# Value columns leave the seven-product stage normalised, as two planes of 16-bit words that are transposed by DMA when a head loads them

## The chip, the cores and the metric

The kernel runs on one core of a Trainium2 chip. The metric is the device time of one execution in microseconds (us). The core has five engines with queues of their own: TensorE (PE in the profile; its weight loads are PEld), VectorE (DVE), ScalarE (ACT), GpSimd (POOL) and SyncE (SP). An instruction waits at the head of its engine's queue until the semaphores that it names are reached, and what stands behind it waits too. Data moves between DRAM and the on-chip memory SBUF by DMA, which SP, ACT and POOL issue; TensorE's results lie in PSUM.

## The reference

One decoder layer on 1024 tokens of width 2048: a norm, an input projection, eight heads of stick-breaking and eight of differential attention, each gated, an output projection, a gated embedding and a last norm. What the change touches is the norm and the columns v and g:

```python
def rmsnorm(x, g, eps=NORM_EPS):
    xf = x.astype(jnp.float32)
    y = xf * lax.rsqrt(jnp.mean(xf * xf, axis=-1, keepdims=True) + eps)
    return (y * g.astype(jnp.float32)).astype(x.dtype)
...
        hn = rmsnorm(h, norm_mix_g[i])
        proj = hn @ w_in[i]
        sb_q, sb_k, sb_v, sb_g, df_q, df_k, df_v, df_g = jnp.split(proj, split_at, axis=-1)
...
        sb_out = stick_breaking_attention(sb_q.reshape(sb_shape), sb_k.reshape(sb_shape),
                                          sb_v.reshape(sb_shape)).reshape(B, S, SB_WIDTH)
...
        mixed = jnp.concatenate([sb_out * jax.nn.silu(sb_g), df_out * jax.nn.silu(df_g)], axis=-1)
```

The factor rsqrt(mean of squares) belongs to a token, so it can be multiplied into a projected column after the product.

## The kernel before

Products are made in float32 precision from pairs: every operand is split into a high part, rounded to TensorE's float format (a copy on ScalarE), and the rest (a subtraction on VectorE), and each 128x128 by 128x512 product takes three passes: high by high, high by low, low by high. "High" and "low" below mean these parts.

**The v and g columns** (4096 of the 8192) are computed first, transposed: a unit u is one head, with 128 columns of v and 128 of g, for two halves of 512 tokens. This 2x2 block product is made with seven products instead of eight, named by their operands: A11, A12, S2, S1, S3, A22, S4 (class `Seven`, L656). The x operands (tiles cA11, cS2 and so on, 512 tokens wide) stay for all units; the weights' sums (T1 to T4, L760) are made for each unit on VectorE, then rounded on ScalarE (L801) and their low parts taken on VectorE (L815), one weight for each product made, in a fixed order (`step`). The contraction over 2048 runs in two passes: `ph` 0 takes half of x's rows for all 16 units, `ph` 1 the other half. In the first pass, the A11 and A12 products of all units come first, by themselves, up to about 95 us; then 16 units of five products, to about 312 us; then the second pass, 16 units of seven, to about 613 us. A unit's results are sums (s1, u2, u3: L1145 to L1170) and come out as four tiles of 128 columns by 512 tokens, for token halves `hf` and for v (`blk` 0) or g (`blk` 1). `vput` (L913) stores them on GpSimd's DMA queue into vg_d; in the second pass that DMA adds to what lies there. So vg_d ends with unnormalised v and g, columns on partitions. `prod` (after each product) also runs small pieces of other work from a list `gv.xq`, each from a given slot (number of products) on, two or three at most for a product.

**Visits.** Behind each of the first four units of the first pass, `visit(i)` (L997) loads four x tiles `xv` of the other half of x's rows (both token halves of two blocks) and leaves their combinations in DRAM for the second pass, in two pieces: `one` (slot + 3) scales a tile on ScalarE (L1014) and makes two combinations, `two` (slot + 5) two more. The four tiles are those of a ring, so a visit's loads, on SyncE's queue, wait until the stores of the visit before have landed.

**Row sums of squares.** In every second unit of the second pass, `squares` (L1050) loads four x tiles on ScalarE's DMA queue and, in two pieces, squares them on ScalarE and adds them into `ssa`, one tile for each token half (L1066). The sums over partitions are made later, in the first steps of the attention stage: `split_sum` (L1223) and `norms` (L1210), with four ssps products, a logarithm and an exponential for each half (`rstd_from`, L113) and three VectorE rows, which leave the factor in `ssa`, the same in each partition.

**Attention** runs over half 1 and then half 0 of the tokens, and over 16 heads in each. For each head a stream of projection products for q and k (L294 to L296, accumulators acc) runs on TensorE with the pieces of attention between them; a counter `side` decides after which product a piece is issued (the table TICK). `load_vg` (L1441) loads vf and gf, 256 KB each, from vg_d; `normed(0)` and `normed(1)` multiply them by the factor (L1464); `values` (L465) transposes vf on TensorE in four blocks of 128 tokens (vps, L472), and makes v's high part (L474, ScalarE) and low part (L477, VectorE). The softmax weights are transposed by TensorE too (tp, L492), split into high and low (lead, awh, awl), and multiplied with v (av).

The two pieces of a visit, and the transposes of v, are these:

```python
            def one():
                A.activation(b2, b2, AF.Copy, scale=gcol(kb))
                V.scalar_tensor_tensor(b2, a2, gcol(ka), b2, op0=ALU.mult, op1=ALU.add)
                store("S1", b2)
                V.tensor_tensor(a2, a2, a1, op=ALU.subtract)
                store("S3", a2)
...
            for j in range(4):
                T.transpose(vps[:, j, :], vg[0][:, j * P:(j + 1) * P], ident)
```

Of the kernel before, what the change touches and what calls it, by code (L numbers as in the profile page):

```python
# [15 lines left out]
BF16 = mybir.dt.bfloat16  # L16
AF = mybir.ActivationFunctionType
# [28 lines left out]
    (1, 2), "kv": 9, "df_vg": (25, 37, 42, 58, 59.5), "sb_vg": (4, 15, 16, 24, 25.5), "q_turn": (-1.0, 5.5, 5, 6.5, 10, 12,  # L46
# [22 lines left out]
def _body(ctx, nc, tc, ap):  # L69
# [236 lines left out]
    vg_d = dram.tile([2, 2, NVG, P, HALF], F32, name="vg_d", tag="vg_d")  # L306
    h_d = dram.tile([2, NK, P, HALF], F32, name="h_d", tag="h_d")
# [37 lines left out]
    def attention(at, pz, half, hd, q, qz, K, KL, VV, sg, vg, rcol):  # L345
# [119 lines left out]
        def values():  # L465

            if sb:
                vps = pz.tile([P, 8, P], F32, name="vps", tag="z")[:, 0:4, :]
            else:
                vps = pp.tile([P, 4, P], F32, name="vps", tag="t")  # L470
            for j in range(4):
                T.transpose(vps[:, j, :], vg[0][:, j * P:(j + 1) * P], ident)  # L472
            v = at.tile([P, 2, 4, P], F32R, name="v", tag="v")
            side.later(TICK["vparts"][0], lambda: A.copy(v[:, 0], vps))  # L474

            def low():
                V.tensor_tensor(v[:, 1], vps, v[:, 0].bitcast(F32), op=ALU.subtract)  # L477
# [154 lines left out]
    with tc.tile_pool(name="at", bufs=2) as at, tc.tile_pool(name="pz", bufs=2, space=PSUM) as pz:  # L632
# [370 lines left out]
        def visit(i):  # L1003
# [8 lines left out]

            def one():
                A.activation(b2, b2, AF.Copy, scale=gcol(kb))  # L1014
                V.scalar_tensor_tensor(b2, a2, gcol(ka), b2, op0=ALU.mult, op1=ALU.add)
# [10 lines left out]
            return one, two  # L1026
# [26 lines left out]
        def squares(n):  # L1053
            ts = []
            for j in range(4):
                t = spare()
                A.dma_start(t, xsrc(j % 2, 2 * n + j // 2))
                ts.append(t)

            def some_of(j0):  # L1060
                for j in (j0, j0 + 1):
                    if n == 0 and j < 2:
                        A.activation(ssa[j % 2], ts[j], AF.Square)
                    else:
                        A.activation(ts[j], ts[j], AF.Square)
                        V.tensor_tensor(ssa[j % 2], ssa[j % 2], ts[j], op=ALU.add)  # L1066

            return partial(some_of, 0), partial(some_of, 2)
# [57 lines left out]
        def rest_of(st_, first):  # L1126
# [6 lines left out]
            vput(o, ph, hf, blk, u)  # L1133
# [3 lines left out]
        for ph in range(2):  # L1137
            for u in range(NVG):
# [69 lines left out]
        rstds = {}  # L1208

        def norms():  # L1210
            t = ev.tile([P, HALF], F32, name="ssq", tag="ssq")
            for hf in (1, 0):
                ps = pp.tile([P, HALF], F32, name="ssps", tag="t")
                high, low = halves[hf]
                T.matmul(ps, onesr, high, start=True, stop=False)
                T.matmul(ps, onesr, low, start=False, stop=True)
                side.later(1 if hf else 3, partial(rstd_from, ps, 1.0 / NK, eps6, EPS, ssa[hf], t))
                rstds[hf] = ssa[hf]
            with tc.issue_after(gv.lastx.ins):
                consts_late()  # L1220

        halves = {}

        def split_sum(hf):
            high, low = halves[hf] = [ev.tile([P, HALF], F32R, name=nm, tag="xt", bufs=4) for nm in ("ssah", "ssal")]
            A.copy(high, ssa[hf])
            V.tensor_tensor(low, ssa[hf], high.bitcast(F32), op=ALU.subtract)

        side.add([(14 - hf, partial(split_sum, hf)) for hf in (1, 0)] + [(18, norms)])
# [199 lines left out]
        for half in (1, 0):  # L1429
            X = X0 if half == 0 else X1  # L1430

            for hd in ORDER:
# [8 lines left out]
                def load_vg(vg=vg, hd=hd, half=half):  # L1441
                    for i in range(2):
                        vg.append(f32t(("vf", "gf")[i]))
                        nc.sync.dma_start(vg[i], vg_d[half, i, hd])
# [101 lines left out]
                if half == 0:  # L1546
# [3 lines left out]
                    def load_kv(k2=k2, v2=v2, KL=KL, hd=hd):  # L1550
                        G.dma_start(k2.rearrange("p a b -> p (a b)"), k_d[hd])
                        if hd >= H:
# [7 lines left out]
                                                   (load_vg, partial(normed, 0), partial(normed, 1), gate, gated))])  # L1560
# [877 lines left out]
```

## Time and profile before

| | |
|---|---|
| three runs | 2318.01, 2314.68, 2315.53 us, median 2315.53 |
| span of the profiled execution, first to last instruction | 2312.5 us |
| its own time, with some 3 us around the span | 2315.5 us |
| granted TensorE clock, mean | 0.999 |
| busy in the span: TensorE, VectorE, ScalarE, GpSimd | 100%, 78%, 55%, 14% |
| DMA traffic | 556.66 MB, mean 241 GB/s |

A row of a timeline gives the start in us, the duration in us, engine, source line, operation, output<-inputs, shape and count, and in brackets the idle time of the engine just before and what ended it. A group row gives minimum, median and maximum duration in ns, and the first and last start. Matmuls overlap in the array: starts are 0.23 us apart where each shows 0.39. VectorE's and ScalarE's rows overlap by some 0.1 us as well, so the start of the next row tells what one costs its engine.

### The profile page before, as it was taken

How to read it: one execution, taken by the hardware profiler on the slowest of the kernel's cores; microseconds unless marked ns; L12 is line 12 of the kernel's file. 1: busy time of each engine (PE TensorE's matmuls, PEld its weight loads, DVE VectorE, ACT ScalarE, POOL GpSimd, SP SyncE). 2: the span in 40 equal slices, each digit the busy share in tenths (PEclk: the TensorE clock that was granted, in tenths of full speed). 3: DMA queues.
4: the chain of work that ended last, by engine and by line, in shares of the span. 5: the costliest groups of instructions: out<-in, count | busy, mean ns of one | idle time of the engine just before them, and what ended most of it. 6: DMA issues, size and time to landing. Idle time of an engine off the chain costs nothing.

```text
span 2312.5 us, 32656 instructions
## 1 busy us (share of the span) xinstructions
PE 2301.0 (100%) x11089; PEld 1928.8 (83%) x11089; DVE 1800.0 (78%) x3123; ACT 1273.0 (55%) x2308; POOL 329.8 (14%) x498
## 2 busy tenths in 40 slices
PE   9999999999999999999999999999999999999998
PEld 7888888888888888888888888888888888888887
DVE  6587776766678888878778878788887988687887
ACT  6423243433356677778776766667733435542555
POOL 2121111111211111101011001110121121111000
PEclk9999999999999999999999999999999999999999
DMA  7687788876887787889676667777899789998975
GB/s 268 215 296 234 253 280 226 213 160 131 207 273 253 244 255 247 252 286 309 196 214 188 184 202 210 203 203 241 264 214 246 248 246 283 308 354 275 301 259 187
DMA packets 258455, 556.66 MB, mean 241 GB/s; under 512 B 28896, under 2 KB 39392, under 8 KB 258288
## 3 DMA queue, kind: packets, MB, share of 16 engines
q1 hardware_dynamic: 180816, 366.55, 49.9%
q0 software_dynamic: 60912, 158.10, 26.1%
q10 hardware_dynamic: 16560, 29.92, 3.5%
q8 instruction: 87, 1.43, 0.2%
q14 instruction: 80, 0.66, 0.1%
HBM read 359.16 MB, written 203.69 MB: 243 GB/s over the span
## 4 chain that ended last, share of the span: by engine, by line
PE 97%; DVE 1%; issue 0%; ACT 0%; DMA 0%; SPq 0%; DVEq 0%; ACTq 0%
PE pbc L706 14%; PE pa L706 11%; PE acc L294 10%; PE acc L296 10%; PE acc L295 10%; PE pc L706 9%; PE pb L706 4%; PE tp L492 3%; PE pb L1856 2%; PE pb L1854 2%; PE pb L1855 2%; PE av L539 1%; PE z L386 1%; PE z L385 1%; PE av L538 1%; PE av L537 1%
## 5 line engine op out<-in xcount | busy, mean ns | idle before, releaser
L801 ACT CAST wpr<-T 128x512 fp32r<-128x512 f32 x208 | 127.1, 621 | 469.0 <-DVE T L760 392.9
L294 PE MATMUL acc<-xh,whi 128*128 128x512 f32 x768 | 312.3, 407 | 0.0
L296 PE MATMUL acc<-xh,wlo 128*128 128x512 f32 x768 | 301.1, 392 | 0.0
L295 PE MATMUL acc<-xl,whi 128*128 128x512 f32 x768 | 300.7, 392 | 0.0
L296 PEld LDWEIGHTS acc<-xh,wlo 128*128 128x128 f32 x768 | 144.2, 188 | 32.3 <-DVE wlo L195 0.2
L294 PEld LDWEIGHTS acc<-xh,whi 128*128 128x128 f32 x768 | 144.7, 188 | 24.2
L295 PEld LDWEIGHTS acc<-xl,whi 128*128 128x128 f32 x768 | 144.9, 189 | 23.7
L914 POOL DMA_DIRECT2D vg_d<-hc x128 | 89.8, 701 | 444.8 <-DVE hc L1132 263.2
L815 DVE TENSOR_TENSOR wpr<-T,wpr 128x512 fp32r<-128x512 f32 x208 | 142.7, 686 | 7.2 <-ACT wpr L801 4.2
L199 ACT CAST whi<-wraw 128x1024 fp32r<-128x1024 f32 x128 | 134.1, 1048 | 17.0 <-DMA wraw<-w_in 7.6
L801 ACT CAST wpr<-wraw 128x512 fp32r<-128x512 f32 x128 | 78.7, 618 | 103.6 <-DMA wraw<-tw_d 33.7
L441 ACT ACTIVATE et<-z,mx 128x512 f32<-128x512 f32 (+7 forms) x128 | 95.2, 744 | 59.1 <-DVE mx L433 58.9
L433 DVE CUSTOM_DVE_ANT_0 z<-z,wide 128x512 f32<-128x512 f32 (+7 forms) x128 | 97.7, 765 | 32.7 <-PE z L386 29.3
L516 DVE TENSOR_TENSOR awl<-tp,awh 128x256 fp32r<-128x256 f32 (+1 forms) x160 | 92.6, 579 | 32.6 <-ACT awh L511 31.7
L706 PE MATMUL pbc<-cA,wpr 128*128 128x512 f32 x480 | 115.5, 390 | 0.3 <-DVE u L1170 0.2
L706 PE MATMUL pbc<-cS,wpr 128*128 128x512 f32 x480 | 115.3, 389 | 0.0
L706 PE MATMUL pc<-cS,wpr 128*128 128x512 f32 x480 | 115.3, 389 | 0.0
L706 PEld LDWEIGHTS pbc<-cA,wpr 128*128 128x128 f32 x480 | 90.0, 188 | 19.7 <-DVE u L1170 0.7
L706 PEld LDWEIGHTS pc<-cS,wpr 128*128 128x128 f32 x480 | 90.1, 188 | 18.7
L706 PEld LDWEIGHTS pbc<-cS,wpr 128*128 128x128 f32 x480 | 90.1, 188 | 18.7
L706 PE MATMUL pbc<-cS2h,wpr 128*128 128x512 f32 x320 | 105.2, 390 | 0.0
L706 PE MATMUL pc<-cS4h,wpr 128*128 128x512 f32 x320 | 105.0, 389 | 0.0
(554 smaller groups left out, 6376.5 us busy)
## 6 DMA issues: line engine op xcount, KB each, us to landing
wraw<-w_in SPq DMA_DIRECT2D x128, 512.0 KB, 4.6
wraw<-w_vg SPq DMA_DIRECT2D x143, 256.0 KB, 3.6
vg_d<-hc POOLq DMA_DIRECT2D x128, 256.0 KB, 5.0
wlo_d<-wlo POOLq DMA_DIRECT2D x56, 512.0 KB, 6.3
wlo<-wlo_d SPq DMA_DIRECT2D x48, 512.0 KB, 4.1
wraw<-w_gate SPq DMA_DIRECT2D x92, 256.0 KB, 5.4
h_d<-hc POOLq DMA_DIRECT2D x56, 256.0 KB, 5.2
wraw<-w_out SPq DMA_DIRECT2D x56, 256.0 KB, 4.7
```

Of the source, the lines that this page charges most:

```text
L199: side.later(1, lambda: A.copy(hi[:, o], raw[:, o]))
L294: T.matmul(acc[c], hi[:, k2, kh, c, :], xh, start=first, stop=False)
L295: T.matmul(acc[c], hi[:, k2, kh, c, :], xl, start=False, stop=False)
L296: T.matmul(acc[c], lo[k2][:, kh, c, :], xh, start=False, stop=last)
L433: V.tensor_tensor_reduce(z[:, vw], z[:, vw], add, -DF_SCALE, 3.0e38, ALU.add, ALU.min, mx)
L441: A.activation(et[:, vw], z[:, vw], AF.Exp, bias=mx[:, 0:1], scale=-1.0, accum_out=l[:, c:c + 1])
L492: T.transpose(tp[:, j, b * P:(b + 1) * P], ws[2 * pr + b][:, (g0 + j) * P:(g0 + j + 1) * P], ident)
L516: V.tensor_tensor(wl[:, o, :], tp[:, o, :], wh[:, o, :].bitcast(F32), op=ALU.subtract)
L706: T.matmul(o, a[:, w], x, start=start and k + i == 0, stop=k == 3 and i == 2, skip_group_check=True)
L801: A.copy(t[:, 0], src)
L815: V.tensor_tensor(t[:, 1], src, t[:, 0].bitcast(F32), op=ALU.subtract)
L914: G.dma_start(vg_d[hf, blk, u], o, **(dict(accum_op=ALU.add) if ph else {}))
```

## The change

1. The squares move. `visit` returns a third piece, `zero`, in the same slot as `one` and ahead of it: four squares of xv on ScalarE, added into `ssa` on VectorE. The other sixteen x tiles are squared by `squares` behind units 7 to 10 of the first pass. None is left in the second pass.
2. The sums over partitions and the norm factors are made at the start of the second pass: `split_sum` ahead of its first product, the ssps products behind it, the `norms` rows behind the second. Small constants (`consts_late`) come in the unit after.
3. In the second pass, a v tile (`blk` 0) is not stored with an adding DMA. The first pass's part is loaded (`load_parts`, two loads of 256 KB per unit on SyncE's queue), added on VectorE, multiplied by `ssa` on VectorE (`finished`), and one product later ScalarE copies its 16-bit words into two planes (`divided`), which are stored plainly into vt_d. The g tiles are as before.
4. A head loads v with a transposing DMA (vf, now 16-bit words with tokens on partitions); two ScalarE copies put the words of the planes together into vw. The transposes on TensorE and `normed(0)` go; high and low parts of v are taken from vw.

```diff
+    vt_d = dram.tile([2, NVG, P, 2 * HALF], U16, name="vt_d", tag="vt_d")
...
-            if sb:
-                vps = pz.tile([P, 8, P], F32, name="vps", tag="z")[:, 0:4, :]
-            else:
-                vps = pp.tile([P, 4, P], F32, name="vps", tag="t")
-            for j in range(4):
-                T.transpose(vps[:, j, :], vg[0][:, j * P:(j + 1) * P], ident)
             v = at.tile([P, 2, 4, P], F32R, name="v", tag="v")
-            side.later(TICK["vparts"][0], lambda: A.copy(v[:, 0], vps))
+            whole = ev.tile([P, 4, P], F32, name="vw", tag="xt", bufs=4)
+            words = whole.bitcast(U16).rearrange("p a (b c) -> p a b c", c=2)
+            planes = vg[0].bitcast(U16).rearrange("p (c a b) -> p c a b", c=2, a=4)
+            for c in range(2):
+                A.copy(words[:, :, :, c], planes[:, c])
+            side.later(TICK["vparts"][0], lambda: A.copy(v[:, 0], whole))
...
+            def zero():
+                for (hf, c), v in t.items():
+                    if i == 0 and c == 0:
+                        A.activation(ssa[hf], v, AF.Square)
+                        continue
+                    s = spare()
+                    A.activation(s, v, AF.Square)
+                    V.tensor_tensor(ssa[hf], ssa[hf], s, op=ALU.add)
...
-            vput(o, ph, hf, blk, u)
+            if ph and first:
+                V.tensor_tensor(o, o, parts_of[u][hf], op=ALU.add)
+                finished(o, hf, u)
+            else:
+                vput(o, ph, hf, blk, u)
...
+        def finished(o, hf, u):
+            V.tensor_tensor(o, o, ssa[hf], op=ALU.mult)
+            planes = parts_of[u][hf].bitcast(U16)
+            words = o.bitcast(U16).rearrange("p (a b) -> p a b", b=2)
+
+            def divided():
+                for c in range(2):
+                    A.copy(planes[:, c * HALF:(c + 1) * HALF], words[:, :, c])
+                G.dma_start(vt_d[hf, u], planes)
+
+            gv.soon.append((gv.slot + 1, divided))
...
+                    if u == 0:
+                        split_sum(1)
+                        split_sum(0)
                     a = pp.tile([P, HALF], F32, name="pa", tag="acc", bufs=2)
                     prod(u, ph, "A11", a, True)
                     A.copy(s1, a)
-                    if prev:
-                        rest_of(prev, True)
+                    if u == 0:
+                        total(1)
+                        total(0)
+                    rest_of(prev, True)
+                    if u == 0:
+                        norms()
+                    load_parts(u)
...
-                    A.copy(o, a)
-                    vput(o, ph, 1, 0, u)
+                    V.tensor_tensor(o, a, parts_of[u][1], op=ALU.add)
+                    finished(o, 1, u)
...
-                if ph and u % 2 == 0:
-                    gv.xq.extend((gv.slot + 3, fn) for fn in squares(u // 2))
+                if ph == 0 and u in range(7, 11):
+                    gv.xq.extend((gv.slot + 3, fn) for fn in squares((2, 3, 6, 7)[u - 7]))
...
-                    one, two = visit(u)
-                    gv.xq.extend([(gv.slot + 3, one), (gv.slot + 5, two)])
+                    zero, one, two = visit(u)
+                    gv.xq.extend([(gv.slot + 3, zero), (gv.slot + 3, one), (gv.slot + 5, two)])
...
-                    for i in range(2):
-                        vg.append(f32t(("vf", "gf")[i]))
-                        nc.sync.dma_start(vg[i], vg_d[half, i, hd])
+                    vg.extend(f32t(nm) for nm in ("vf", "gf"))
+                    nc.sync.dma_start_transpose(vg[0].bitcast(U16).rearrange("p (a b) -> p a b", b=P), vt_d[half, hd])
+                    nc.sync.dma_start(vg[1], vg_d[half, 1, hd])
```

How the instructions stand in the queues, at three places. (Line numbers are those of each kernel.)

VectorE at the second visit (the unit u = 1 of the first pass), before: the scaling's reader L1015 stands right behind the S4 weight (L813), and behind it T1, T2 (L760) and the low parts (L815), of which the last is S2's.

```order
L813 SCALAR_TENSOR_TENSOR wpr<-wraw,wpr 128x512
L1015 SCALAR_TENSOR_TENSOR xv<-xv,gvec 128x512
L1017 TENSOR_TENSOR xv<-xv 128x512
L760 TENSOR_TENSOR T_1216<-wraw 128x512
L760 TENSOR_TENSOR T_1219<-b_847,T_1216 128x512
L815 TENSOR_TENSOR wpr<-T_1192,wpr 128x512
L1132 TENSOR_TENSOR hc<-pc,u_1039 128x512
L815 TENSOR_TENSOR wpr<-T_1219,wpr 128x512
```

The same place of VectorE after the change:

```order
L814 SCALAR_TENSOR_TENSOR wpr<-wraw,wpr 128x512
L1021 TENSOR_TENSOR ssa<-ssa,spare 128x512 x4
L1025 SCALAR_TENSOR_TENSOR xv<-xv,gvec 128x512
L1027 TENSOR_TENSOR xv<-xv 128x512
L761 TENSOR_TENSOR T_1234<-wraw 128x512
L761 TENSOR_TENSOR T_1237<-b_848,T_1234 128x512
L816 TENSOR_TENSOR wpr<-T_1200,wpr 128x512
L1139 TENSOR_TENSOR hc<-pc,u_1040 128x512
L816 TENSOR_TENSOR wpr<-T_1237,wpr 128x512
```

Four adds are now ahead of the scaling's reader; on ScalarE, four squares stand likewise right ahead of the scaling (L1014 before, L1024 now).

VectorE where the second pass begins, before: hc<-pbc is the result of A22 of the first pass's last unit, behind it comes a weight's low part and the splits of the operand cS.

```order
L1132 TENSOR_TENSOR hc<-pbc,s_2684 128x512
L815 TENSOR_TENSOR wpr<-T_2855,wpr 128x512
L689 SCALAR_TENSOR_TENSOR cS_2823<-cS_2823,gvec 128x512
L689 SCALAR_TENSOR_TENSOR cS_2825<-cS_2825,gvec 128x512
L1157 TENSOR_TENSOR u_2916<-pbc,s_2841 128x512
```

The same place after the change:

```order
L1139 TENSOR_TENSOR hc<-pbc,s_2778 128x512
L116 SCALAR_TENSOR_TENSOR nt<-ssps,ssa 128x512
L117 SCALAR_TENSOR_TENSOR nt<-nt,ssa 128x512
L118 SCALAR_TENSOR_TENSOR ssa<-nt,ssa 128x512
L116 SCALAR_TENSOR_TENSOR nt<-ssps,ssa 128x512
L117 SCALAR_TENSOR_TENSOR nt<-nt,ssa 128x512
L118 SCALAR_TENSOR_TENSOR ssa<-nt,ssa 128x512
L816 TENSOR_TENSOR wpr<-T_2957,wpr 128x512
L690 SCALAR_TENSOR_TENSOR cS_2917<-cS_2917,gvec 128x512
L690 SCALAR_TENSOR_TENSOR cS_2919<-cS_2919,gvec 128x512
L1220 TENSOR_TENSOR u_3039<-pbc,s_2935 128x512
```

The six rows of the norms are new here; the two of `split_sum` (ssal) stand eight rows further ahead.

ScalarE in the first head of attention, before: et are softmax rows, whi a projection weight, lead and awh the high parts of transposed softmax weights.

```order
L199 CAST whi<-wraw 128x1024
L441 ACTIVATE et,l<-z,mx 128x256
L510 CAST lead<-tp 128x128
L511 CAST awh<-tp 128x256
L474 CAST v<-vps 128x512
L441 ACTIVATE et,l<-z,mx 128x256
```

The same place after the change:

```order
L200 CAST whi<-wraw 128x1024
L443 ACTIVATE et,l<-z,mx 128x256
L474 COPY vw<-vf 128x512 x2
L511 CAST lead<-tp 128x128
L512 CAST awh<-tp 128x256
L475 CAST v<-vw 128x512
L443 ACTIVATE et,l<-z,mx 128x256
```

The two copies of words stand ahead of lead and awh. On SyncE, the load of vf stands where it stood, as a transposing DMA.

More of the change, by code (lines that the diff above doesn't have):

```diff
@@ L16 @@
 BF16 = mybir.dt.bfloat16
+U16 = mybir.dt.uint16
 AF = mybir.ActivationFunctionType
@@ L1024, in two @@
                 store("S4", b1)
-            return one, two
+            return zero, one, two
         spares = []
@@ L1132, in rest_of, with split_sum, total, norms @@
             V.tensor_tensor(o, o_, t, op=ALU.add)
-            vput(o, ph, hf, blk, u)
+            if ph and first:
[3 more added lines that the diff above has]
+                vput(o, ph, hf, blk, u)
+        rstds, halves, totals = {}, {}, {}
+        def split_sum(hf):
+            high, low = halves[hf] = [ev.tile([P, HALF], F32R, name=nm, tag="xt", bufs=4) for nm in ("ssah", "ssal")]
+            A.copy(high, ssa[hf])
+            V.tensor_tensor(low, ssa[hf], high.bitcast(F32), op=ALU.subtract)
+        def total(hf):
+            ps = totals[hf] = pp.tile([P, HALF], F32, name="ssps", tag="t" if hf else "acc", bufs=2)
+            high, low = halves[hf]
+            T.matmul(ps, onesr, high, start=True, stop=False)
+            T.matmul(ps, onesr, low, start=False, stop=True)
+        def norms():
+            t = ev.tile([P, HALF], F32, name="nt", tag="xt", bufs=4)
+            for hf in (1, 0):
+                rstd_from(totals[hf], 1.0 / NK, eps6, EPS, ssa[hf], t)
+                rstds[hf] = ssa[hf]
+        parts_of = {}
+        def load_parts(u):
+            if u:
+                t = at.tile([P, 2, HALF], F32, name="part", tag="qz")
+                parts_of[u] = [t[:, i, :] for i in range(2)]
+            else:
+                parts_of[u] = [ev.tile([P, HALF], F32, name="part", tag="xt", bufs=4) for _ in range(2)]
+            for hf in (1, 0):
+                nc.sync.dma_start(parts_of[u][hf], vg_d[hf, 0, u])
+        def finished(o, hf, u):
[7 more added lines that the diff above has]
+            gv.soon.append((gv.slot + 1, divided))
         late = deque(partial(divide, "S4", i) for i in (2, 3))
@@ L1207, in _body @@
         side.add([(t, gv.xq.popleft()[1]) for t in GVT[-len(gv.xq):]])
[L1208 to L1229, printed above, removed]
         rcols = {}
```

15 lines of the change are left out of this document (7 added, 8 removed).

## The prediction

> **What bounds the kernel now.** I read the page first: busy time by engine, then the chain that ended last.
>
> ```profile
> PE 2301.0 (100%) x11089; PEld 1928.8 (83%) x11089; DVE 1800.0 (78%) x3123; ACT 1273.0 (55%) x2308; POOL 329.8 (14%) x498
> PE 97%; DVE 1%; issue 0%; ACT 0%; DMA 0%; SPq 0%; DVEq 0%; ACTq 0%
> PE warm L919 <- POOL eps L92: 1.0, 1, 1.0
> PE ssps L2244 <- DVE sq L2217: 0.7, 1, 0.7
> ```
>
> TensorE works in all of the span, and the chain runs through it. The last two lines, from the list of what TensorE waited for, are its longest waits: 1.0 us at the start, 0.7 at the end. So whatever leaves TensorE is gained in full, unless another engine then makes it wait; and whatever makes it wait anywhere is lost in full. The other engines matter only by their slack, so next comes the table by stage (busy times; the first window is the part of the first pass in which the x tiles are visited, the second the seam between the passes, the third the second pass, the others the two halves of attention):
>
> ```profile
> core 0: us, PE busy (x) PEld busy (x) DVE busy (x) ACT busy (x) POOL busy (x), PEclk, DMA share, GB/s
> 95.00:165.00 70.00, 69.75 (x308) 57.42 (x308) 60.00 (x94) 19.78 (x35) 16.77 (x31) 1.00 0.79 265
> 312.00:346.00 34.00, 34.00 (x151) 28.16 (x151) 25.89 (x42) 16.91 (x30) 5.43 (x7) 1.00 0.86 247
> 346.00:613.00 267.00, 266.98 (x1178) 220.83 (x1178) 174.28 (x272) 96.80 (x173) 52.31 (x62) 1.00 0.76 181
> 613.00:1085.00 472.00, 471.60 (x2336) 395.10 (x2335) 383.70 (x793) 323.17 (x647) 67.98 (x113) 1.00 0.85 267
> 1085.00:1650.00 565.00, 564.94 (x3047) 484.52 (x3046) 452.50 (x791) 402.05 (x691) 60.43 (x82) 1.00 0.72 212
> ```
>
> VectorE is 86% busy (60.00 of 70) just where the change puts the new squares and adds, 76% (25.89 of 34) at the seam, where it puts the norms, and 65% (174.28 of 267) in the pass after, where it takes squares away. The clock is 1.00 throughout and cannot give or take anything.
>
> **What goes: the transposes of v.** The groups of the tile vps, and one of them in TensorE's timeline:
>
> ```profile
> L472 PE MATMUL vps<-ident,vf x128: 270/272/274, 673.5 to 1635.7; 128*128 128x128 f32 x128
> 673.01 0.39 PE L295 MATMUL acc<-cA12l,whi 128*128 128x512 f32 x1
> 673.23 0.40 PE L296 MATMUL acc<-cA12h,wlo 128*128 128x512 f32 x1
> 673.47 0.60 PE L472 MATMUL vps<-ident,vf 128*128 128x128 f32 x4
> 673.82 0.48 PE L294 MATMUL acc<-cA12h,whi 128*128 128x512 f32 x1
> 674.14 0.39 PE L295 MATMUL acc<-cA12l,whi 128*128 128x512 f32 x1
> ```
>
> A transpose shows 272 ns, but they overlap, so the price is read from the starts around a group. Ordinary products start 0.23 us apart (673.01 to 673.23). From 673.23 to 674.14 there are 0.91 us; two steps of 0.23 would be 0.46, so a group of four costs 0.45 us. There are 128/4 = 32 groups: **-14.3 us** (32 x 0.446, the mean gap by the same starts). The four ssps products move from attention's first half to the seam at an unchanged price, 0.
>
> **What is added in the first pass.** At each of the first four units the chore `zero` squares all four x tiles on ScalarE and adds them on VectorE, ahead of `one`. First the last load of the second visit and of the fourth, each with its landing, and two groups of all four visits; then rows of the second visit from three timelines:
>
> ```profile
> L1007 SPq DMA_DIRECT2D xv<-xT x1: 328/328/328, 121.3 to 121.3; - x1
> DMA to landing us min/median/max: 4.6/4.6/4.6
> L1007 SPq DMA_DIRECT2D xv<-xT x1: 328/328/328, 148.6 to 148.6; - x1
> DMA to landing us min/median/max: 3.9/3.9/3.9
> L1007 SPq DMA_DIRECT2D xv<-xT x16: 327/328/442, 47.6 to 148.6; - x16
> L1015 DVE SCALAR_TENSOR_TENSOR xv<-xv,gvec x4: 752/752/752, 110.4 to 151.5; 128x512 f32<-128x512 f32 x4
> 122.70 0.62 ACT L801 CAST wpr<-T 128x512 fp32r<-128x512 f32 x1 [3.09 <-DVE T L760]
> 123.23 0.72 ACT L1014 ACTIVATE xv<-xv,gvec 128x512 f32<-128x512 f32 x1
> 123.98 0.75 DVE L1015 SCALAR_TENSOR_TENSOR xv<-xv,gvec 128x512 f32<-128x512 f32 x1 [0.77 <-ACT xv L1014]
> 126.09 0.69 DVE L760 TENSOR_TENSOR T<-b,T 128x512 f32<-128x512 f32 x1
> 126.70 0.69 DVE L815 TENSOR_TENSOR wpr<-T,wpr 128x512 fp32r<-128x512 f32 x1
> 127.91 0.69 DVE L815 TENSOR_TENSOR wpr<-T,wpr 128x512 fp32r<-128x512 f32 x1
> 129.73 0.62 PE L706 MATMUL pb<-cS2h,wpr 128*128 128x512 f32 x2
> ```
>
> The fourth tile is loaded last, at 121.3, and lands 4.6 us later, at 125.9. Before, only `two` needed it, at 129. Now its square is ahead of the scaling of L1014 on ScalarE. ScalarE starts instructions 0.53 us apart (122.70 to 123.23): square at 126.0, scaling at 126.5, its reader L1015 at 127.3 instead of 123.98, **3.3 us late**. Behind L1015 on VectorE stand T1 and T2, and behind these S2's weights, whose low half ended at 128.6 (127.91 + 0.69) for the third product at 129.73: slack 1.14 us. So TensorE waits some 3.3 - 1.14 = 2.2 us. By the same slack: the first visit (loads from 47.6 on, long landed at 110.4) is late by four squares, 4 x 0.53 = 2.1, and waits 1.0. The fourth's last tile lands at 148.6 + 3.9 = 152.5, so L1015 moves from 151.5 to 153.8, 2.3 late, a wait of 1.2. For the third I take the mean of its neighbours, 1.7. Together 6.1. The adds of L1021 cost VectorE 0.61 each (126.09 to 126.70), 14 of them 8.5 us, most in the time in which VectorE waits for ScalarE; but u3 and `two`'s rows behind them come later too, and the next unit's loads wait for these stores. I add 3 us, a third of those 8.5. The first pass: **+9 us**, bounds 3.4 (only the second and the fourth visit wait) and 14.6 (6.1 + 8.5). The 16 squares after unit 7 come with no waiter behind them but VectorE's queue: +0.5.
>
> **The seam.** VectorE's idle time when the second pass begins, and S2's weights with the product that reads them in a later unit:
>
> ```profile
> 312.67 0.69 DVE L1132 TENSOR_TENSOR hc<-pbc,s 128x512 f32<-128x512 f32 x1
> 317.77 1.42 DVE L689 SCALAR_TENSOR_TENSOR cA<-spare,gvec,cA 128x512 fp32r<-128x512 f32 x2 [0.69 <-ACT cA L683]
> 325.86 0.69 DVE L1170 TENSOR_TENSOR u<-pbc,s 128x512 f32<-128x512 f32 x1 [1.13 <-PE pbc L706]
> ...
> 424.49 0.69 DVE L815 TENSOR_TENSOR wpr<-T,wpr 128x512 fp32r<-128x512 f32 x1
> 426.75 0.61 PE L706 MATMUL pbc<-cS2h,wpr 128*128 128x512 f32 x2
> ```
>
> Between 312.67 and 325.86 it is idle 0.69 + 1.13 = 1.8 us. Into this stretch come six rows of the norms, right behind the first of these lines (0.7 each, 4.2), and an add and a multiply (1.2); the two ssal rows stand just ahead. 5.4 - 1.8 = 3.6 us more than fits before u3 at 325.86 is ready; the six also wait for the ssps products and two logs and exponentials on ScalarE. Behind u3 stand S2's weights for the next unit; in a later unit they end 426.75 - 425.18 = 1.6 us ahead of their reader, and that takes part of it. **+4 us**; below, 2 (3.6 less that slack), above, 6 (3.6 and a wait of about 2.4, four ScalarE rows, for the exponentials).
>
> **The second pass.** In each unit VectorE gets four rows (two adds of `part`, two multiplications), 16 x 4 = 64, and loses 30 adds of squares: 34 x 0.61 = 21 us on 267 us, of which it was idle 93. ScalarE gets four copies and loses one, and two squares. The two 256 KB loads of `part` and the plain stores take the place of two accumulating stores, and the squares' loads go. A VectorE queue at 73% hides this except where a chore's rows fall together: **+1.5**, bounds 0 and 5.
>
> **Attention.** ScalarE gets two copies of 16-bit words per head and half, VectorE loses the row that normalised vf. The load must be in time for the copies, which stand at the place of the transposes:
>
> ```profile
> L1444 SPq DMA_DIRECT2D vf<-vg_d x32: 319/326/1227, 646.3 to 1612.0; - x32
> DMA to landing us min/median/max: 2.5/4.4/9.3
> 720.75 0.38 SPq L1444 DMA_DIRECT2D vf<-vg_d  x1
> 739.72 0.60 PE L472 MATMUL vps<-ident,vf 128*128 128x128 f32 x4
> 675.37 0.27 ACT L510 CAST lead<-tp 128x128 fp32r<-128x128 f32 x1 [1.71 <-PE tp L492]
> ```
>
> (The landing is that of all the rows of vf.) The load issued at 720.75 is used at 739.72, 19 us later; the first has 27 us (646.3 to 673.5). A transposed load is in no trace here. Of the same 256 KB, its landing is bounded by 2.5 us below and, with no row that excludes it, by more than that cover above; I take 4.4 to 9.3, the rows' median and maximum, and both cost nothing. The two copies (0.53 each by the starts above, bounded by 0.3 and 1.2) fall into 1.71 us that ScalarE waits ahead of `lead`. But TensorE's work is now 0.45 us shorter there, so the others have that much less time: **+1**, bounds -1 (VectorE is 32 x 0.6 = 19 us lighter) and +14 (all is given back).
>
> The Trainium skill speaks against such a step: "VectorE: DVE Perf Modes", section "The three transpose paths", has 390 ns for a 128x128 transpose on TensorE and 1309 ns by DMA. By it the eight 16-bit blocks of a load would be an estimated 8 x 1.309 = 10.5 us, against 4 x 0.39 = 1.6 us on TensorE. The trace has 0.45 us for the latter, and no run here shows the former; inside 19 us of cover it would still cost nothing. "Advanced Engine Details and Errata", section "DGE: Hardware vs Software", rates the transposes of the hardware queues worse than those of the software queues; that belongs to the third rival below.
>
> **Sum**, against the profiled execution (span 2312.5 and about 3 around it, which gives 2315.5, the median of the runs shown): -14.3 + 9 + 0.5 + 4 + 1.5 + 1 = +1.7, so **2317.2 us**. By the terms' ends, 2315.5 - 14.3 + 3.4 + 2 + 0 - 1 = 2305.6 to 2315.5 - 14.3 + 14.6 + 0.5 + 6 + 5 + 14 = 2341.3.
>
> **Rivals.**
> 1. The slack takes it. The visits wait 3.4, the seam costs 2, the rest nothing: 2315.5 - 14.3 + 5.4 = 2306.6. For it: VectorE still has 10 of 70 us idle in the visits. Against it: the reader of L1014 is late by a landing time, which no idle VectorE makes up. Chance 0.27.
> 2. Attention gives the gain back: ScalarE's copies delay a softmax row that VectorE and then TensorE's tp products wait for, at 32 places by the 0.45 us saved there. 2317.2 + 13 = 2330. For it: VectorE is 81% busy there (383.70 of 472) and TensorE's cover shrinks. Against: ScalarE is at 68% and VectorE loses a row. It decides where the two copies take more than 1.71 - 0.45 = 1.26 us, or where ScalarE has no such wait. Chance 0.18.
> 3. The transposed loads are slow. From 19 us of landing the copies wait, and so does SyncE's queue, which also brings w_in. At 1 us late per load, 32 us: 2317 + 32 = 2349. Chance 0.11.
>
> The forecast keeps 0.44, with a range of its own of 2311 to 2324. A measurement here tells some 0.2% (4.6 us) from no change: faster is under 2310.9, slower over 2320.1. Faster 0.28 (rival 1 and a little of the forecast's), same 0.36, slower 0.36 (rivals 2 and 3 and 0.07 of the forecast's). The range, 2304 to 2338, leaves out the third rival and a tail below.
>
> **What would show it.** Right: TensorE's list of waits has new entries on wpr or T at 115 to 160 us of 1 to 2.5 us each and at 315 to 335 us, and two neighbours of each former vps group stand 0.23 us apart. Wrong in the first pass: no wait on S2's weights there. Wrong in attention: waits of TensorE on awh or lead with ScalarE's word copies ahead of them, or copies that start only when vf lands. The number falls most with the visits: if VectorE's adds block more than a third of their time, it is too low.

## The result, and the profile after

The kernel after the change takes 2332.9 us (median of four runs, 2331.8 to 2336.9) against 2315.1 us before on the same chip (2314.5 to 2318.0): ratio 1.0078, 95% interval 1.0064 to 1.0092, slower by 17.8 us. The forecast was 2317.2 with a range of 2304 to 2338: the range holds the time, but the forecast itself was 15.7 us too low, and the range of its own (2311 to 2324) does not hold it.

The page of the profile after the change (its span is 18.4 us longer than before), and the list of what TensorE waited for (engine, tile and line, in total us, times, longest), in its longest rows:

```profile
PE 2295.7 (98%) x10961; PEld 1915.7 (82%) x10961; DVE 1818.6 (78%) x3155; ACT 1336.7 (57%) x2420; POOL 320.8 (14%) x498
PE 56%; DVE 8%; ACT 5%; issue 2%; DMA 1%; DVEq 0%; ACTq 0%; POOL 0%; POOLq 0%
PE av L535 <- DVE lead L516: 6.7, 9, 1.0
PE pbc L707 <- ACT wpr L802: 3.9, 3, 2.1
PE pbc L707 <- DVE u L1233: 2.6, 3, 1.3
PE av L540 <- DVE awl L517: 2.4, 10, 0.6
PE pa L707 <- DVE wpr L816: 2.1, 1, 2.1
PE acc L295 <- ACT qk L1549: 1.4, 6, 0.2
PE z L381 <- ACT et L443: 1.2, 1, 1.2
PE ssps L1157 <- DVE ssal L1151: 1.1, 2, 0.8
```

TensorE is busy 5.3 us less; that is not the 14.3 of the transposes, since busy time counts slowed products too and hides some 0.16 us of each wait (a product that the list has 1.04 us late is 1.20 late from start to start). The chain that ended last, which was TensorE for 97%, is so for 56% and also goes through VectorE and ScalarE. Where two waits of before were 1.0 and 0.7 us, there are now many, in three places: the visits and the seam (wpr, u, ssps), and attention (lead, awl, qk).

To place the loss in time, I matched each product with the same product before and took the difference of their starts; how that delay grows within a stretch is what the stretch costs. The stretches are in the time of before: the first products (0 to 95 us), the visits (95 to 165), the rest of the first pass (to 308), the seam (to 350), the second pass (to 613), attention's start, where the ssps products used to be (to 634), half 1 (to 1084), half 0 (to 1640), and the rest. The table has the change and all experiments below, each against the same trace of before:

| | first | visits | to 308 | seam | second pass | to 634 | half 1 | half 0 | rest | span |
|---|---|---|---|---|---|---|---|---|---|---|
| the change | 0.2 | 9.5 | 0.0 | 8.0 | 1.6 | -0.5 | 2.9 | -4.9 | 1.7 | +18.4 |
| e1 | 0.2 | 10.3 | 0.0 | 7.4 | 2.6 | -0.5 | -5.6 | -6.2 | 1.2 | +9.4 |
| e2 | 1.1 | 9.6 | 0.0 | 7.0 | 1.6 | -0.5 | -5.0 | -6.0 | 1.7 | +9.5 |
| e3 | 0.5 | 0.0 | 0.1 | 13.6 | 1.5 | -0.5 | 2.8 | -4.6 | 2.8 | +16.2 |
| e4 | 1.1 | 7.5 | 0.0 | 6.5 | 1.7 | -0.5 | 2.9 | -4.9 | 3.0 | +17.3 |
| e5 | 1.4 | 12.2 | 1.0 | 1.4 | 1.9 | -0.5 | 2.9 | -4.8 | 1.5 | +17.1 |
| e6 | 0.3 | 0.0 | 5.4 | 7.3 | 1.7 | -0.5 | 2.9 | -4.4 | 4.0 | +16.7 |
| e7 | 0.6 | 0.0 | 3.9 | 0.7 | 1.4 | -0.5 | -3.6 | -4.5 | 4.2 | +2.2 |
| e8 | 0.3 | 11.4 | 0.0 | 6.6 | 0.6 | -0.5 | 2.9 | -4.9 | 2.0 | +18.4 |
| e9 | 0.6 | 13.3 | 1.4 | 0.6 | 0.4 | -0.5 | -3.1 | -3.2 | 1.2 | +10.7 |
| e10 | 1.7 | -0.3 | 2.4 | 0.6 | 1.0 | -0.5 | -3.5 | -4.4 | 1.1 | -2.0 |

Kernels that leave a stretch as it was agree there within 1.5 us, except in the visits (9.5 to 12.2 with `zero` unchanged), the second pass (0.4 to 2.6) and the rest (1.1 to 4.2). Each row is one execution.

Part of that spread is TensorE's granted clock. After the change it is not 1.00 throughout, as the stretch of the seam shows (the columns are those of the table by stage in the prediction, where this stretch has 1.00):

```profile
312.00:346.00 34.00, 30.77 (x125) 24.16 (x125) 30.71 (x50) 19.30 (x35) 3.60 (x6) 0.95 0.83 287
```

The clock was 0.5 there for 3.4 us, from 341.9, a microsecond after a wait of 2.1 us. Products then started 0.43 us apart instead of 0.23, and that cost 1.6 us. The same happened once in the seam of e1, e4, e6 and e8, for 6.8 us in that of e3 (some 3 us), once in the visits of e1 and e9 and twice in those of e5 (some 3 us), in half 0 of e9, and from 7.6 to 11.0 us in e10; between the first 12 us and the last 10, the kernel before, e2 and e7 have none. Each began within 2 us of the end of a wait, but waits of up to 3.4 us (e4) passed without it, so what sets it off is not shown. Without these stretches the visits with `zero` unchanged cost 8.7 to 9.6.

The second visit after the change, from the timelines of ScalarE, VectorE and TensorE:

```profile
127.03 0.63 ACT L1020 ACTIVATE spare<-xv 128x512 f32<-128x512 f32 x1 [0.38 <-DMA xv<-xT]
127.57 0.71 ACT L1024 ACTIVATE xv<-xv,gvec 128x512 f32<-128x512 f32 x1
128.31 0.75 DVE L1025 SCALAR_TENSOR_TENSOR xv<-xv,gvec 128x512 f32<-128x512 f32 x1
131.88 0.50 PE L707 MATMUL pb<-cS2h,wpr 128*128 128x512 f32 x1 [1.04 <-ACT wpr L802]
132.98 0.73 PE L707 MATMUL pb<-cS2h,wpr 128*128 128x512 f32 x2 [0.37 <-DVE wpr L816]
```

The last square waits for its tile to land, the scaling follows, and TensorE waits for both parts of S2's weights. The four visits cost 1.2, 2.0, 2.5 and 3.8 us.

The transposes are gone, but the two halves of attention are shorter by 2.9 - 4.9 = -2.0 us only, and not by 14.3.

The groups of the new tiles, from the views of the tiles vw and vf after the change:

```profile
L474 ACT COPY vw<-vf x64: 752/766/794, 691.7 to 1653.6; 128x512 uint16<-128x512 uint16 x64
L1484 SPq DMA_TRANSPOSE vf<-vt_d x32: 1232/1498/5213, 665.0 to 1628.5; - x32
DMA to landing us min/median/max: 3.0/4.8/10.0
```

A word copy takes 0.77 us. The transposed load lands like the plain one (4.8 against 4.4 in the median, 10.0 against 9.3 at most), though its issue holds SyncE 1.5 us, where the plain load's took 0.33.

The copies in a stick-breaking head, ScalarE's timeline after the change:

```profile
757.46 0.37 ACT L443 ACTIVATE et<-z,mx 128x128 f32<-128x128 f32 x1 [1.70 <-DVE mx L435]
757.73 0.19 ACT L443 ACTIVATION_READ_ACCUMULATOR et<-z,mx 128x1 f32 x1
757.82 1.38 ACT L474 COPY vw<-vf 128x512 uint16<-128x512 uint16 x2
759.22 1.28 ACT L267 ACT_TABLE_LOAD   x1
760.51 0.63 ACT L1508 ACTIVATE sg<-gf 128x512 f32<-128x512 f32 x1
```

And VectorE there, with the row that it waits for and a row 20 us on:

```profile
761.18 0.69 DVE L1511 TENSOR_TENSOR sg<-sg,gf 128x512 f32<-128x512 f32 x1 [2.87 <-ACT sg L1508]
...
780.55 0.27 DVE L516 TENSOR_TENSOR lead<-tp,lead 128x128 fp32r<-128x128 f32 x1
```

The two copies stand right behind a softmax row for which ScalarE had waited 1.70 us, and ahead of the table load and the gate sg; so it is in seven of the eight such heads of half 1. So VectorE waits 2.87 us for sg. Before, that wait was 1.58:

```profile
741.07 0.69 DVE L1470 TENSOR_TENSOR sg<-sg,gf 128x512 f32<-128x512 f32 x1 [1.58 <-ACT sg L1467]
```

Behind it VectorE has next to no gap until the low part of lead, which is then late for TensorE (0.95 us here, 6.7 in the list).

### The profile page after: what moved, and what is told of

The parts are those of the page before. It is cut to its first block, busy times and chain, and to the rows that moved or that the text cites. A ratio compares the mean times of both kernels' runs of the same rounds, so it can differ in the third digit from the quotient of the medians.

```text
span 2331.0 us, 32671 instructions
## 1 busy us (share of the span) xinstructions
PE 2295.7 (98%) x10961; PEld 1915.7 (82%) x10961; DVE 1818.6 (78%) x3155; ACT 1336.7 (57%) x2420; POOL 320.8 (14%) x498
## 4 chain that ended last, share of the span: by engine, by line
PE 56%; DVE 8%; ACT 5%; issue 2%; DMA 1%; DVEq 0%; ACTq 0%; POOL 0%; POOLq 0%
PE acc L295 7%; PE acc L297 7%; PE acc L296 7%; PE pbc L707 5%; PE pc L707 3%; PE pa L707 2%; DVE pt L418 2%; PE tp L493 2%; PE pb L707 2%; PE pb L1897 2%; PE pb L1895 2%; PE pb L1896 2%; PE pc L1897 1%; PE pc L1896 1%; PE pc L1895 1%
## 5 line engine op out<-in xcount | busy, mean ns | idle before, releaser
L512 ACT CAST awh<-tp 128x256 fp32r<-128x256 f32 (+1 forms) x160 | 80.8, 505 | 39.0 <-PE tp L493 38.8
```

What stands on the lines that cost most here:

```text
L512: A.copy(wh[:, o, :], tp[:, o, :])
```

## The experiments

**e1: without the word copies.**

```diff
-            whole = ev.tile([P, 4, P], F32, name="vw", tag="xt", bufs=4)
-            words = whole.bitcast(U16).rearrange("p a (b c) -> p a b c", c=2)
-            planes = vg[0].bitcast(U16).rearrange("p (c a b) -> p c a b", c=2, a=4)
-            for c in range(2):
-                A.copy(words[:, :, :, c], planes[:, c])
+            whole = vg[0].bitcast(BF16).rearrange("p (c a b) -> p c a b", c=2, a=4)[:, 1]
```

> The kernel after the change, without the two copies of 16-bit words on ScalarE: v is read from the plane of its high words alone, so v is less exact. The transposed loads stay. The profile after the change has 64 such copies of 766 ns, and TensorE, which gained some 14 us from the transposes, lost about 13 of them again in attention. Theory A, the copies delay ScalarE's rows behind them and so VectorE and TensorE: attention (615 to 1660 us of the trace) gets 9 to 13 us shorter, time 2320 to 2324. Theory B, the transposed loads (1.5 us of SyncE's queue each instead of 0.33) or the shorter cover do it: less than 3 us, 2330 or more.

2322.7 us, ratio to before 1.0028 (1.0013 to 1.0042). Attention went from -2.0 to -11.8 us; nothing else moved by more than 1. The copies are the cause, and v's high and low parts take as long as with them (0.61 and 0.68 us); with the transposed loads still there, these and the shorter cover have at most 14.3 - 11.8 = 2.5 us.

**e2: the copies of the stick-breaking heads earlier.** They become a step of their own, three groups of products ahead of the former place.

```diff
+        def joined():
+            whole = ev.tile([P, 4, P], F32, name="vw", tag="xt", bufs=4)
...
+        steps.append((20 if sb else tv, joined))
         steps.append((tv, values))
```

> The kernel after the change, with the two word copies of a stick-breaking head three products' groups earlier, so that they fall into the 1.7 us in which ScalarE waits for a softmax row, ahead of that row instead of behind it and ahead of the table load and the gate. Nothing is left out. Theory A (place of the copies): the wait of about 1 us at lead in each pair of the first half goes, 8 pairs, and some 0.5 us more at the q and k copies: 8 to 11 us less, 2322 to 2325. Theory A' (the copies' sheer time on ScalarE, wherever they stand): less than 4 us. Theory B (loads): nothing.

2324.4 us, ratio 1.0039 (1.0025 to 1.0053); attention -11.0. ScalarE at the same place (the softmax row starts 1.4 us earlier in this kernel):

```profile
754.30 1.41 ACT L474 COPY vw<-vf 128x512 uint16<-128x512 uint16 x2
756.10 0.37 ACT L443 ACTIVATE et<-z,mx 128x128 f32<-128x128 f32 x1 [0.39 <-DVE mx L435]
756.36 0.19 ACT L443 ACTIVATION_READ_ACCUMULATOR et<-z,mx 128x1 f32 x1
756.57 1.28 ACT L267 ACT_TABLE_LOAD   x1
```

The same two copies, of the same 1.4 us, now stand in the wait for mx, of which 0.39 us is left. It was the place of the copies, not their time: 9.0 of the 9.8 us that e1 gained are there with the copies still made, and half the copies (the differential heads') were not moved at all. Nearly all of it is in half 1 (7.9 us); in half 0 the softmax row ahead of the copies had not waited.

**e3: no squares in the visits.** `zero` goes, and `squares` runs for all eight blocks:

```diff
-                if ph == 0 and u in range(7, 11):
-                    gv.xq.extend((gv.slot + 3, fn) for fn in squares((2, 3, 6, 7)[u - 7]))
+                if ph == 0 and u in range(7, 15):
+                    gv.xq.extend((gv.slot + 3, fn) for fn in squares(u - 7))
```

> The kernel after the change, but all 32 squares are made from tiles of their own behind units 7 to 14 of the first pass, and none in the visits. Theory: the visits cost what the trace shows as TensorE's delay between 113 and 165 us, 9.5 us, and blocks of squares behind later units cost nothing (0.03 us between 165 and 308): 2323 to 2324. Rival: the adds cost VectorE's time wherever they stand in the first pass, as it is over 80% busy there: 2328 or more.

A miss: 2330.5 us, the rival's time but not in its place. The visits' 9.5 us went to 0.0, so `zero` is all of that term, and the blocks cost 0.1. But the seam grew from 8.0 to 13.6, of which some 3 are the clock. TensorE's timeline there:

```profile
314.24 0.50 PE L1150 MATMUL ssps<-ssah,onesr 128*128 128x512 f32 x1 [4.19 <-DVE cS2l L688]
316.18 0.79 PE L1151 MATMUL ssps<-ssal,onesr 128*128 128x512 f32 x1 [1.44 <-DVE ssal L1145]
```

The ssps products wait until VectorE has come past an operand's split and then for ssal, and A22 stands behind them in TensorE's queue.

**e4: the late tile taken out.** The tiles that `one` overwrites are squared ahead of it, the other two (the last to land) ahead of `two`.

```diff
+            def two():
+                zero(1)
...
-            return zero, one, two
+            return partial(zero, 0), one, two
```

> The kernel after the change, but in a visit only the two tiles that `one` overwrites are squared ahead of it, and the other two (the last to land) ahead of `two`. As many squares and adds as before. Theory L (the fourth tile's late landing holds ScalarE, and the scaling behind it): the delay between 113 and 165 us falls from 9.5 to 3 or 4 us, time about 2327. Theory Q (the adds in VectorE's queue are the cost): it stays at 8 or more, 2331 or more.

2332.0 us; the visits cost 7.5 instead of 9.5. Nearer to theory Q, and the waits moved. The list of TensorE's waits of this kernel between 100 and 200 us has only:

```profile
PE pbc L707 <- DVE u L1236: 5.1, 3, 3.4
PE pb L707 <- DVE u L1236: 0.9, 1, 0.9
```

No wait on S2's weights is left; u, which stands behind `two` in VectorE's queue, is late instead, by up to 3.4 us. Against the 8.7 to 9.6 of the kernels with `zero` unchanged, the landing of the fourth tile is worth 1 to 2 us, in one profile of each; the rest is the new rows, wherever they stand in the unit.

**e5: norm factors in the first pass.**

```diff
+                if ph == 0 and u == 12:
+                    gv.xq.extend((gv.slot + 5, partial(split_sum, hf)) for hf in (1, 0))
+                if ph == 0 and u == 13:
+                    gv.xq.extend((gv.slot + t, partial(fn, hf)) for t, fn, hf in ((1, total, 1), (1, total, 0), (2, norms, 1), (4, norms, 0)))
...
-                    if u == 0:
-                        split_sum(1)
-                        split_sum(0)
...
-                    if u == 0:
-                        total(1)
-                        total(0)
...
-                    if u == 0:
-                        norms()
```

> The kernel after the change, but the sums over partitions and the norm factors are made in the first pass (splits behind unit 12, ssps products and the VectorE rows behind unit 13, the factors of the two halves two products apart) instead of at the start of the second; the small side products on SyncE's queue pause four slots longer for it. The squares stay in the visits and behind units 7 to 10. Theory: the seam's delay (308 to 350 us, 8.0 us, of which 0.9 are the four products themselves) is made by the norm's eight rows standing in VectorE's queue among the operand splits: it falls to 2 or 3 us, time about 2328. Rival: VectorE has no room in the first pass either, and the delay shows at units 13 to 15 instead: 2331 or more.

2329.9 us. The seam went from 8.0 to 1.4, with 1.0 in the first pass, which is the products themselves (0.9): the seam's theory holds. The total fell by less than 5: in the profiled execution (2331.4 us, the other took 2328.4) the visits cost 12.2, with the clock at 0.5 twice, and the first products 1.2 more than after the change.

**e6: blocks of squares three units earlier than in e3** (behind units 4 to 11).

> As e3_no_zero, but the blocks of squares stand behind units 4 to 11 instead of 7 to 14. In e3 the visits' delay was gone (0.0 us), but the seam's rose from 8.0 to 13.7. Theory: blocks behind the last units push the operand splits of the second pass back in the list of small pieces; with three units between, the seam is back at 8 us and the time at 2323. Rival: without squares in the visits the seam costs more wherever the blocks stand (less slack is left by earlier stalls): 2328 or more.

A miss again in the total, 2329.6, with both halves of the theory to be read apart: the seam is back at 7.3, but 5.4 us appear between the visits and the seam, in steps at 173, 201 and 214 us of before's time. The blocks begin where the operands loaded behind units 4 to 6 (`load_x`) are split, and both are VectorE's rows. In e3 the same blocks, without that company, cost 0.1. That it is this company is argued from the places; e10 has none of the three steps.

**e7: e2, e5 and e6 together.**

> Squares behind units 4 to 11 (e6), norm factors in the first pass (e5), word copies of the stick-breaking heads earlier (e2). Nothing is left out. If the three costs are separate, they add up: 2333 less 9.5 (visits), 5 (seam) and 8.5 (word copies) is 2310, some 0.2% below the kernel before the change. If they share VectorE's slack, a part comes back elsewhere: 2313 to 2320.

2313.45 us (ten runs), ratio 0.9992 (0.9982 to 1.0001): no different from before, and at the lower end of what was expected if the costs share slack. The visits (0.0) and the seam (0.7) gain in full. Of the 3.9 us up to 308, 0.9 are the ssps products and the rest e6's collisions. Attention comes to -8.1 where e2 had -11.0: some 3 us of the word copies' gain are missing, at the end of each half, and so they are in e10 (-7.9) and, without its clock stretch, in e9. All three join e2 with e5, which alone costs attention nothing; why the two together do stays open.

**e8: e4 with the visits' adds on GpSimd.**

```diff
-                    V.tensor_tensor(ssa[hf], ssa[hf], s, op=ALU.add)
+                    G.tensor_tensor(ssa[hf], ssa[hf], s, op=ALU.add)
```

> As e4_zero_split, but the adds of the visits' squares run on GpSimd, which was busy 14% of the span, instead of VectorE. The squares themselves stay on ScalarE, the blocks behind units 7 to 10 as after the change. e4 left 7.5 of 9.5 us of delay in the visits. Theory Q (the adds in VectorE's queue are what is left): the delay between 113 and 165 us falls to 2 us or less, time about 2326. Rival S (ScalarE's four squares ahead of its own rows): it stays at 5 or more, 2330.

2333.1 us, visits 11.4: theory Q fails, and rival S has the number (5 or more) without the reason. The rows of GpSimd and VectorE in the second visit, and one group of all four:

```profile
125.76 3.05 POOL L1023 TENSOR_TENSOR ssa<-ssa,spare 128x512 f32<-128x512 f32 x2 [1.15 <-ACT spare L1022]
127.70 1.66 DVE L1029 TENSOR_TENSOR xv<-xv 128x512 f32<-128x512 f32 x1
132.49 2.12 DVE L1034 SCALAR_TENSOR_TENSOR xv<-xv,gneg 128x512 f32<-128x512 f32 x1
L1029 DVE TENSOR_TENSOR xv<-xv x4: 692/1658/1666, 113.1 to 161.3; 128x512 f32<-128x512 f32 x4
```

VectorE's rows that fall on GpSimd's adds take 1.66 instead of 0.69 and 2.12 instead of 0.75 us. Ten rows, all with both inputs in SBUF, are stretched so, by 9.4 us together, where the 14 adds at 0.61 would have cost VectorE 8.5. Others that meet an add keep their time (126.92, 0.75), among them the rows that read PSUM (hc<-pc,u at 171.28, inside an add, 0.69). So the adds were not taken from VectorE but paid there in another form, and how the rest of the visits' cost divides between ScalarE's squares and VectorE's adds stays open.

**e9: e8's adds for all squares, with e2 and e5.**

> e8 with all adds of squares on GpSimd, the word copies of the stick-breaking heads earlier (e2) and the norm factors in the first pass (e5). Nothing is left out. If the visits' delay is 2, the seam's and the later first pass's 3, the second pass's 1.5, and attention gains 11 to 12 us, then 2315.5 + 6.5 - 11.5 + 1 = 2311 to 2312; each of these costs may come back by 1 or 2 us.

2324.2 us, ratio 1.0035 (1.0024 to 1.0047): a miss by 12. The visits cost 13.3 where 2 were expected, for the same reason and with 1.6 of the clock, and attention came to -6.3, not to -11 or -12: 1.6 went to the clock and some 3 as in e7.

**e10: e7 with the squares spread.** Two blocks stand among the first products, six behind units 7 to 12.

```diff
+                if blocks:
+                    blocks.popleft()()
+                elif i == 1 and u in (4, 8):
+                    blocks.extend(squares(u // 4 - 1))
...
-                if ph == 0 and u in range(4, 12):
-                    gv.xq.extend((gv.slot + 3, fn) for fn in squares(u - 4))
+                if ph == 0 and u in range(7, 13):
+                    gv.xq.extend((gv.slot + 3, fn) for fn in squares(u - 5))
```

> As e7_all_three, but two of the eight blocks of squares stand among the first pass's A11 and A12 products (loaded behind units 5 and 9, squared two units later), and the other six behind units 7 to 12. Nothing is left out. In e7 and e6 the delay between 165 and 308 us was 4.0 and 5.4 us, at the units in which blocks and the splits of loaded operands (behind units 4 to 6) fall together; in e3, with blocks behind units 7 to 14, it was 0.1. Theory (collisions of VectorE's extra rows within a unit): the delay falls to about 1, of which 0.9 are the ssps products, and the time to about 2310.5, ratio 0.998. Rival: VectorE or ScalarE has no room among the first products either, and the delay appears before 95 us: 2313 or more.

2310.15 us (eight runs, 2308.8 to 2314.7), ratio 0.9977 (0.9966 to 0.9987): faster than both kernels, with nothing left out. Between 165 and 308 us 2.4 are left, above the 1 expected. The first products cost 1.7, but all of it before 12 us, in a wait and a clock stretch, ahead of the first square at 51.7; the squares among them cost nothing. Its page and the first waits of its list, all in attention but for u:

```profile
PE 2289.5 (99%) x10961; PEld 1916.0 (83%) x10961; DVE 1820.6 (79%) x3155; ACT 1337.9 (58%) x2420; POOL 320.1 (14%) x498
PE av L541 <- DVE lead L522: 2.3, 7, 1.2
PE av L546 <- DVE awl L523: 2.1, 4, 1.2
PE pbc L714 <- DVE u L1231: 1.5, 2, 1.1
```

VectorE and ScalarE are as busy as after the change (1820.6 and 1337.9 against 1818.6 and 1336.7 us): the 22.8 us are won by places, with the same rows on both engines and sixteen more loads of x.

## Why the prediction was right in its range and wrong in its middle

The range held because it took in rival 2. The forecast's own terms give 2317 and not 2333, and the size of its first-pass term is in part luck.

- **The transposes, -14.3.** Right as a price: a step of -0.36 us, and -0.09 at the next product, together the 0.45, stands at each former group in the difference of the two traces, before the waits that follow.
- **The first pass, +9.5 (9 and 0.5).** Measured 9.5 in the visits and 0.0 behind unit 7. The size was right, the mechanism only in part: by visit, 1.0, 2.2, 1.7 and 1.2 us and 3 for the adds were forecast, and 1.2, 2.0, 2.5 and 3.8 came. The reader of the scaled tile was late as worked out (3.3 us forecast): it starts at 128.31, where 123.98 before and a delay of 1.4 by then make 125.4, so 2.9 late. But taking the late tile away (e4) gained 1 to 2 us only. The prediction had this as the small part, "a third of those 8.5"; the rows in the queue weigh more than the landing.
- **The seam, +4.** Mis-sized: 8.0, less 0.9 for the products that moved there (paid back at 631 us, in the column to 634) is 7.1, beyond the upper bound of 6; without the 1.6 us at half clock it is 5.5, inside it. "The clock is 1.00 throughout and cannot give or take anything" held for the kernel before, not for the one after. The sum counted VectorE's six rows against its idle time up to u3, as one wait. It left out that the ssps products wait for ssal in TensorE's own queue (1.1 us in the list, 1.9 from start to start), and behind that two more waits come one after another: a weight's low part, the `pa` row of the list (2.1), and u (0.9, at 365 us).
- **The second pass, +1.5.** Measured 1.6.
- **Attention, +1.** This step failed; it was 14.3 - 2.0 = 12.3. The prediction took a word copy at 0.53 us, from starts of rows that were not 16-bit copies, with a bound of 1.2; two take 1.4 together, past the 1.26 us at which it said rival 2 decides. And it rested on one place, the differential head, where ScalarE waits 1.71 us ahead of lead. There the copies are nearly harmless (e2 leaves them in place and is 0.8 us behind e1). The cost came from the stick-breaking heads, 10.0 us of it in half 1, where the copies stand behind the wait and ahead of a table load. Rival 2 had the kind of loss (a gain given back through ScalarE and VectorE) and its size (2330), with 0.18; it named lead as the place of the cover, and lead is where the wait showed, the sign that the prediction had named, 20 us behind its cause. e1 and e2 show it.
- **The transposed loads** (rival 3) cost nothing that TensorE's list shows; the most that e1 leaves for them is 2.5 us.
- **The slack** (rival 1) did not take it: with the extra rows in the visits no run had less than 7.5 there.

Together: 9.5 + 0.0 + 7.1 + 1.6 + 12.3 - 14.3 = 16.2, and 2.3 us in the first products (0.2), attention's start (0.4) and behind 1640 us (1.7, on the waits of attention's last products), where kernels with the same code differ by as much. The runs on record lie 1.7 to 1.9 us above their spans, not 3; the forecast started from the median, so that costs it nothing.

## What to carry to other kernels

When work moves off the engine that bounds a kernel onto one that follows it, look at each kind of place that it lands in: in half 1 the same two copies cost next to nothing in one head and about 1 us in the next, depending on whether they stand in front of a wait or behind it. A move by a few steps, into a gap that the timeline already shows, gave back 9 us without changing an instruction. Extra rows on a busy engine were nearly free in units that had no other extra rows (0.1 us for e3's eight blocks) and not where they met others, and moving them to an engine that slowed it down while it worked was no help.

## What the runs showed of the hardware

ScalarE's copy of 128x512 16-bit words to every second word takes 0.77 us, longer than the 0.63 us of a square of as many floats. A transposing DMA of 256 KB lands in 4.8 us in the median (3.0 to 10.0), like a plain load (4.4), and holds the issuing queue 1.2 to 5.2 us. The Trainium skill, "VectorE: DVE Perf Modes", section "The three transpose paths", gave 1309 ns for a 128x128 block, an estimated 10.5 us for the eight of a load; the trace's median is less than half.

An add of 128x512 floats on GpSimd takes 1.30 us in the median (1.29 to 1.82), and VectorE's rows with two SBUF operands stretch from 0.69 to 1.66 us beside it, while a row that reads PSUM keeps its 0.69. The same page of the Trainium skill, section "Two Vector instructions with no wait between them", says that GpSimd shares VectorE's second read interface to SBUF; the rows agree, though no run here separates that from another cause.

A wait of TensorE can cost more than itself: the granted clock fell to 0.5 for 3.4 us, 1.6 us of work, within 2 us of the end of some waits and not of others.
